# Weight parts written six chunks ahead of an item instead of four (jobs not counted), and the splits of output tiles queued behind the newest parts

## The chip, the cores and the metric

The kernel runs on one core of a Trainium2 chip. The metric is the device time of one execution in microseconds. Three runs of the kernel before gave 2260.38, 2260.41 and 2262.13 us; the median is 2260.41.

The engines are named as in the profile: PE is TensorE (matmuls), with its weight loads shown apart as PEld; DVE is VectorE, ACT is ScalarE, POOL is GpSimd and SP is SyncE, which here only issues DMAs. Each engine works through its own instructions in the order in which they were queued. An instruction that waits holds back all that stands behind it on that engine.

## The reference

Two residual layers on 256 tokens of width 2048, all in float32. The first mixes tokens by neighbourhood attention, the second by a short gated convolution; each is followed by a gated MLP with a convolution of three taps ahead of the gate.

```python
def short_conv_mixer(x, w_in, conv_w, w_out):
    gb, gc, h = jnp.split(x @ w_in, 3, axis=-1)
    return (gb * dwconv_centered(gc * h, conv_w)) @ w_out
...
def conv_glu_ffn(x, w_up, conv_w, conv_b, w_down):
    h = dwconv_centered(x @ w_up, conv_w) + conv_b
    g, u = jnp.split(h, 2, axis=-1)
    return (jax.nn.silu(g) * u) @ w_down
...
    for i in range(DEPTH):
        m, j = i % N_MIXERS, i // N_MIXERS
        a = rms_norm(h, mix_norm[i])
        if m == 0:
            mixed = neighborhood_attention(a, na_w_qkv[j], na_rpb[j], na_w_o[j])
        elif m == 1:
            mixed = short_conv_mixer(a, sc_w_in[j], sc_conv_w[j], sc_w_out[j])
...
        h = h + mixed
        h = h + conv_glu_ffn(rms_norm(h, ffn_norm[i]), ffn_w_up[i], ffn_conv_w[i],
                             ffn_conv_b[i], ffn_w_down[i])
    return rms_norm(h, final_norm)
```

## The kernel before

**Numbers as two parts.** A float32 value goes through PE as the sum of two parts in the type fp32r: `hi` is the value cast down, `lo` is the rest. A weight chunk is 128x1024 numbers (512 KB). It is loaded by SP into a `raw` buffer (line 164), cast on ACT into `hi` (line 185) and subtracted on DVE into `lo` (line 188). There are six buffers each of `raw`, `hi` and `lo`. Each activation tile is split in the same way by `split_into` (ACT cast at line 294, DVE subtraction at line 295).

**Phases.** `Phase` computes products whose output is laid out features by tokens: the q and k columns (`wqk`), the short convolution's inputs (`wsc`), and the MLP's up projections (`wup`), in two halves for each layer. An item is a pair of output tiles, of four chunks in all. PE does 32 matmuls on `hi` (line 262, 512 columns, since both parts of the activation lie side by side) and 32 on `lo` (line 270, 256 columns). When a tile's sum is complete, `evac` takes it out of PSUM: ACT copies half of it (line 315), DVE adds and scales (lines 316 and 321), then come the convolution (ACT line 329, twice DVE line 331), for the first tile of a pair the gate's Silu (ACT line 735), for the second the product (DVE line 738), and the split of the product (lines 294 and 295). `Tokens` computes the products whose output is laid out tokens by features (`wo`, `wscout`, `wdown`), with a scheme of seven products in place of eight for some blocks. That scheme needs sums of activations, which `make_forms` computes on POOL (lines 516 to 519) and splits, and sums of weights.

**Jobs.** The sums of weights are made ahead of time, in the phases before: a job loads three tiles (SP), adds them (DVE, lines 207 to 209) and stores three sums to DRAM (ACT queue, line 214). Jobs stand in the list of chunks between the chunks of the pairs, one behind most pairs of a phase from an early pair on (`hosts`). They count as one chunk each.

**What sets the order.** The main loop goes through the items. `prep_to(n)` writes down load, cast and subtraction of all chunks up to number n. Before an item it is called up to the item's last chunk; after the item, whose `evac` has then been written down, it is called again up to four chunks behind the item's end:

```python
            prep_to(ends[item[0]])
            done = ph.run(ft, c, k0, ka, kb)
...
                prep_to(ends[item[0]] + AHEAD)
```

A scheduler then builds the queue of each engine from this text: an instruction that was written down earlier goes first where several could run by the scheduler's own estimate of time, and later ones go ahead where the earlier ones are not ready by that estimate. `tc.issue_after(x)` adds the one rule that an instruction stands behind `x` on the same engine, without a wait. `load` uses it, so that SP's loads keep the order in which they are written down.

Of the kernel before, what the change touches and what calls it, by code (L numbers as in the profile page):

```python
# [15 lines left out]
F32 = mybir.dt.float32  # L16
# [16 lines left out]
QSCALE = float(128 ** -0.5)  # L33

CH = 8
AHEAD = 4

INTRO = 4
STEP = 4
# [40 lines left out]
def trunk(ctx, tc, xT, par, bias, wqk, wv, wo, wsc, wscout, wup, wdown, out):  # L80
    nc = tc.nc
# [42 lines left out]
    ends = []  # L124
    chunks = []
# [4 lines left out]
    def prep_to(n):  # L130
        while len(prepped) < min(n, len(chunks)):
            src, w, kind = chunks[len(prepped)]
            for due in [x for x in stores if x[0] <= len(prepped)]:
                stores.remove(due)
                due[1]()
            if kind == "make":
                make(*src)
                prepped.append(())
                continue
            raw = wp.tile([P, CH * P], F32, name="raw", tag="raw", bufs=RAWS)  # L140
            if kind == "rows":
                load(raw[:, :w], src)
                prepped.append(parts(raw[:, :w]) + (raw,))
                continue

            if kind == "kept":
                t42, left, sums = prepped[-1][2], prepped[-2][2], src()
                load(t42[:, 4 * P:], sums[:, 8 * P:])
                load(raw, sums[:, :8 * P])
                nc.vector.tensor_add(out=t42[:, :4 * P].rearrange("p (f c) -> p f c", f=4),  # L150
                                     in0=t42[:, 4 * P:].rearrange("p (f c) -> p f c", f=4),
                                     in1=left.rearrange("p (f k c) -> p k f c", f=4, c=P)[:, 1])
                prepped.append((parts(raw), parts(t42)))
                continue

            load(raw[:, :4 * w].rearrange("p (f c) -> p f c", f=4), src.rearrange("f p c -> p f c"))
            prepped.append(parts(raw[:, :4 * w].rearrange("p (f k c) -> p f k c", f=4, c=P)) + (raw,))

    def load(out, in_, strict=True):

        with ExitStack() as order:
            if "SP" in newest:
                order.enter_context(tc.issue_after(newest["SP"].ins))
            last = nc.sync.dma_start(out=out, in_=in_)
        if strict:
            newest["SP"] = last

    def parts(r):

        both, low = high_part(r)  # L170
        low()
        return both
# [15 lines left out]
            newest["DVE"] = nc.vector.tensor_sub(out=lv, in0=r, in1=hv.bitcast(F32))  # L188
        return (hi, lo), low

    kept, newest = {}, {}

    def make(w, g, i, sets, strict):

        kept[id(w), g, i] = dst = dp.tile([P, 3, 4 * P], F32, name=f"kept{len(kept)}")
        if len(sets) < 2:
            sets.append([act_tile().bitcast(F32) for _ in range(3)])
        else:
            sets.reverse()
        for x, f, k in zip(sets[-1], (0, 4, 4), (0, 0, 1)):  # L200
            f, k = 8 * g + f, 2 * i + k
            load(x.rearrange("p (f c) -> p f c", f=4), w[f:f + 4, :, k * P:(k + 1) * P].rearrange("f p c -> p f c"), strict)
        l, r, t = sets[-1]

        def adds():
            with tc.issue_after(newest["DVE"].ins):
                nc.vector.tensor_add(out=l, in0=l, in1=r)
                nc.vector.tensor_add(out=r, in0=t, in1=r)
                nc.vector.tensor_add(out=t, in0=l, in1=t)

        def store():
            for n, x in enumerate((l, r, t)):
                with tc.issue_after(newest["ACT"].ins):
                    nc.scalar.dma_start(out=dst[:, n], in_=x)
        stores.append((len(prepped) + ADDS, adds))
        stores.append((len(prepped) + STORES, store))
# [11 lines left out]
    class Phase:  # L228
# [2 lines left out]

        def __init__(self, w, fts, nk, src, evac, intro=0, step=CH, jobs=(), hosts=(0, 1)):
            self.w, self.nk, self.src, self.evac = w, nk, src, evac
            self.ps = {}
            order = [((ft,), [(k0, k0 + step)]) for k0 in range(0, nk, step) for ft in fts[:intro]]
            rest = fts[intro:]

            odd = len(rest) % 2
            order += [(two, [(k0, k0 + CH) for k0 in range(0, nk, CH)])
                      for two in [rest[:odd]] * odd + [rest[i:i + 2] for i in range(odd, len(rest), 2)]]  # L240
            made, (lo, hi) = 0, hosts
            for n, (two, ks) in enumerate(order):
                items.append((self, two, len(chunks), ks[0][0], ks[0][0], ks[-1][1]))
                for ft in two:
                    for k0, k1 in ks:
                        chunks.append((w[ft, :, k0 * P:k1 * P], (k1 - k0) * P, "rows"))
                ends.append(len(chunks))
                while made < min(len(jobs), max(0, -(-len(jobs) * (n + 1 - lo) // (hi - lo)))):
                    chunks.append((jobs[made], 0, "make"))
                    made += 1  # L250

        def run(self, two, c, k0, ka, kb):
            tiles = [[(k, c + (n * (kb - k0) + k - k0) // CH, (k - k0) % CH * P) for k in range(ka, kb)]
                     for n in range(len(two))]

            for n, ft in enumerate(two):
                if n and waiting:
                    tick()
                if ka == 0:
                    self.ps[ft] = pm.tile([P, 2 * S], F32, name="mm", tag="mm")  # L260
                for k, i, o in tiles[n]:
                    nc.tensor.matmul(self.ps[ft], lhsT=prepped[i][0][:, o:o + P], rhs=self.src[k], start=k == 0,  # L262
                                     stop=False)
            for n, ft in enumerate(two):
                if kb - ka > CH:
                    tick()
                    if n:
                        tick()
                for k, i, o in tiles[n]:
                    nc.tensor.matmul(self.ps[ft][:, S:], lhsT=prepped[i][1][:, o:o + P], rhs=self.src[k][:, :S],  # L270
                                     start=False, stop=k == self.nk - 1)
                if kb == self.nk:
                    self.evac(ft, self.ps.pop(ft))
    held, waiting = [], [True]

    later = []
# [4 lines left out]
    item = [0]  # L281
    at = [0]

    def tick():
        due = [x for x in later if x[0] <= at[0]]
        later[:] = [x for x in later if x[0] > at[0]]
        for _, fn in due:
            fn()
        at[0] += 1


    def split_into(hi, lo, src):

        first = nc.scalar.copy(out=hi, in_=src)  # L294
        nc.vector.tensor_sub(out=lo, in0=src, in1=hi.bitcast(F32))  # L295
        return first

    def split(dst, src):
        return split_into(dst[:, :S], dst[:, S:], src)
# [609 lines left out]
    for item[0], (ph, ft, c, k0, ka, kb) in enumerate(items):  # L909

        with ExitStack() as order:
            for x in factor_at:
                order.enter_context(tc.issue_after(x.ins))
            prep_to(ends[item[0]])
            done = ph.run(ft, c, k0, ka, kb)
            if item[0] != KT // STEP * INTRO:

                if done:
                    order.enter_context(tc.issue_after(done.ins))
                prep_to(ends[item[0]] + AHEAD)  # L920
        if item[0] > KT // STEP * INTRO:
            factor_at.clear()
        tick()
# [70 lines left out]
```

## Time and profile before

| | |
|---|---|
| median of three runs | 2260.41 us |
| the profiled execution: own time / span | 2261.52 / 2259.5 us |
| DVE, busy share of the span | 82% |
| ACT, busy share of the span | 58% |
| POOL, busy share of the span | 5% |
| mean granted PE clock | 0.984 |
| HBM traffic, mean | 245 GB/s |

The order of the work over the span: q, k and v with the attention up to some 320 us, `wo` to some 390 us, the first MLP's halves from there to some 1150 us, each an up phase and a `Tokens` phase; the short convolution to some 1500 us; the second MLP to the end. The share of a busy PE is only half an answer, since a PE that runs at a lower clock is busy too. A view by windows gives the granted clock (PEclk) beside the busy time, and a slower clock is also to be seen in the length of a group of equal matmuls.

### The profile page before, as it was taken

The page shows a single profiled execution, that of the slowest core. Times are in us where ns is not written, and L with a number is a line of the kernel's source. Part 1 is how long each engine was busy: PE and PEld are TensorE (multiplying, and loading weights), DVE is VectorE, ACT ScalarE, POOL GpSimd, SP SyncE. Part 2 cuts the span into 40 slices and gives each one's busy share as a digit, 9 for nine tenths or more (in the row PEclk, how much of TensorE's full clock was granted, in tenths as well). Part 3 has the DMA queues.
Part 4 walks back from the last instruction along what each step waited for, and adds up shares of the span by engine and source line. Part 5 has one row for each costly group of instructions (what it writes and reads, how often), then busy time and mean ns, then how long its engine had stood idle before and what let it go on. Part 6 is the DMA issues. An engine that isn't in the chain of part 4 may idle for free.

```text
span 2259.5 us, 33424 instructions
## 1 busy us (share of the span) xinstructions
PE 2197.4 (97%) x11716; PEld 1902.7 (84%) x11716; DVE 1850.5 (82%) x2842; ACT 1303.6 (58%) x1985; POOL 119.1 (5%) x155
## 2 busy tenths in 40 slices
PE   9999999899999979999999999997999999899998
PEld 8888888778888868888888888886888888788886
DVE  8788668779988868988887877886898887788887
ACT  7555555546666645566655554664666655556565
POOL 1000000002100001210000000000010000000000
PEclk9999999999999989999999999998999999899999
DMA  8678556589768859967778886774986786797685
GB/s 291 222 240 269 182 186 216 170 275 303 258 204 261 268 184 347 315 225 233 255 242 288 300 289 222 233 254 146 315 274 190 247 277 208 255 311 254 196 261 168
DMA packets 362072, 555.34 MB, mean 246 GB/s; under 512 B 21680, under 2 KB 249136, under 8 KB 361904
## 3 DMA queue, kind: packets, MB, share of 16 engines
q1 hardware_dynamic: 332880, 502.23, 68.2%
q10 hardware_dynamic: 29024, 50.98, 5.9%
q8 instruction: 92, 1.51, 0.3%
q14 instruction: 76, 0.62, 0.1%
HBM read 500.70 MB, written 52.43 MB: 245 GB/s over the span
## 4 chain that ended last, share of the span: by engine, by line
PE 94%; DVE 3%; ACT 2%; issue 1%; DMA 0%; POOL 0%; SPq 0%; DVEq 0%; ACTq 0%
PE mm L262 41%; PE mm L270 20%; PE mm L454 6%; PE mm L453 6%; PE mm L455 6%; PE mu L453 3%; PE mu L454 3%; PE mu L455 3%; PE mm L679 1%; PE mm L681 1%; PE mm L680 1%; DVE conv L331 1%; PE tr L361 1%; ACT hi L185 1%; DVE lo L188 1%
## 5 line engine op out<-in xcount | busy, mean ns | idle before, releaser
L185 ACT CAST hi<-raw 128x1024 fp32r<-128x1024 f32 (+1 forms) x920 | 915.0, 1011 | 379.1 <-PE mm L455 127.3
L188 DVE TENSOR_TENSOR lo<-raw,hi 128x1024 fp32r<-128x1024 f32 (+1 forms) x856 | 1015.9, 1212 | 131.8 <-ACT hi L185 61.9
L262 PE MATMUL mm<-a,hi 128*128 128x512 f32 x4096 | 979.8, 396 | 51.4 <-ACT hi L185 50.9
L262 PEld LDWEIGHTS mm<-a,hi 128*128 128x128 f32 x4096 | 772.6, 191 | 210.5 <-ACT hi L185 53.2
L270 PEld LDWEIGHTS mm<-a,lo 128*128 128x128 f32 x4096 | 513.3, 192 | 12.1
L270 PE MATMUL mm<-a,lo 128*128 128x256 f32 x4096 | 518.9, 283 | 0.0
L453 PE MATMUL mm<-hi,act 128*128 128x512 f32 x634 | 247.4, 390 | 0.0
L455 PE MATMUL mm<-hi,act 128*128 128x512 f32 x634 | 246.8, 389 | 0.0
L454 PE MATMUL mm<-lo,act 128*128 128x512 f32 x576 | 224.5, 390 | 0.0
L315 ACT COPY corr<-mm 128x256 f32<-128x256 f32 x256 | 91.1, 370 | 207.4 <-PE mm L270 206.4
L331 DVE SCALAR_TENSOR_TENSOR conv<-pad,pt,conv 128x256 f32<-128x256 f32 x384 | 181.6, 479 | 32.3 <-ACT conv L329 28.0
L329 ACT ACTIVATE conv<-pad,pt 128x256 f32<-128x256 f32 x176 | 105.5, 601 | 163.2 <-DVE pad L321 162.1
L316 DVE TENSOR_TENSOR corr<-mm,corr 128x256 f32<-128x256 f32 x256 | 106.5, 416 | 68.8 <-ACT corr L315 68.1
L455 PEld LDWEIGHTS mm<-hi,act 128*128 128x128 f32 x634 | 119.1, 188 | 24.6
L453 PEld LDWEIGHTS mm<-hi,act 128*128 128x128 f32 x634 | 119.1, 188 | 24.4
L454 PEld LDWEIGHTS mm<-lo,act 128*128 128x128 f32 x576 | 108.2, 188 | 21.8
L519 POOL TENSOR_TENSOR s<-conv 128x128 f32<-128x128 f32 x27 | 39.6, 1468 | 1079.2 <-DVE conv L738 1079.2
L295 DVE TENSOR_TENSOR act<-conv,act 128x256 fp32r<-128x256 f32 x88 | 37.2, 423 | 54.5 <-ACT act L294 54.3
L321 DVE TENSOR_TENSOR pad<-corr,rstd 128x256 f32<-128x256 f32 x176 | 73.7, 419 | 0.8
L454 PE MATMUL mu<-lo,sf 128*128 128x512 f32 x180 | 70.1, 389 | 0.0
L455 PE MATMUL mu<-hi,sf 128*128 128x512 f32 x180 | 70.1, 389 | 0.0
L453 PE MATMUL mu<-hi,sf 128*128 128x512 f32 x180 | 70.1, 389 | 0.0
(160 smaller groups left out, 1573.0 us busy)
## 6 DMA issues: line engine op xcount, KB each, us to landing
raw<-in_wup SPq DMA_DIRECT2D x352, 512.0 KB, 5.5
raw<-in_wdown SPq DMA_DIRECT2D x124, 512.0 KB, 4.8
kept<-act ACTq DMA_DIRECT2D x192, 256.0 KB, 4.9
raw<-in_wsc SPq DMA_DIRECT2D x96, 512.0 KB, 5.5
act<-in_wdown SPq DMA_DIRECT2D x156, 256.0 KB, 6.0
raw<-kept SPq DMA_DIRECT2D x64, 512.0 KB, 5.0
raw<-in_wqk SPq DMA_DIRECT2D x56, 512.0 KB, 4.9
raw<-in_wv SPq DMA_DIRECT2D x32, 512.0 KB, 4.4
```

What stands on the lines that cost most here:

```text
L185: newest["ACT"] = nc.scalar.copy(out=hv, in_=r)
L188: newest["DVE"] = nc.vector.tensor_sub(out=lv, in0=r, in1=hv.bitcast(F32))
L262: nc.tensor.matmul(self.ps[ft], lhsT=prepped[i][0][:, o:o + P], rhs=self.src[k], start=k == 0, stop=False)
L270: nc.tensor.matmul(self.ps[ft][:, S:], lhsT=prepped[i][1][:, o:o + P], rhs=self.src[k][:, :S], start=False, stop=k == self.nk - 1)
L315: nc.scalar.copy(out=corr, in_=ps[:, S:])
L316: nc.vector.tensor_add(out=corr, in0=ps[:, :S], in1=corr)
L321: nc.vector.tensor_mul(out=dst, in0=both(ps), in1=rstd)
L329: nc.scalar.activation(c, x[:, 1:S + 1], AF.Identity, scale=w[1], bias=b)
L331: nc.vector.scalar_tensor_tensor(out=c, in0=x[:, tap:tap + S], scalar=w[tap], in1=c, op0=ALU.mult, op1=ALU.add)
L453: nc.tensor.matmul(ps, lhsT=xh, rhs=wh, start=start, stop=False)
L454: nc.tensor.matmul(ps, lhsT=xh, rhs=wl, start=False, stop=False)
L455: nc.tensor.matmul(ps, lhsT=xl, rhs=wh, start=False, stop=stop)
```

## The change

`AHEAD` becomes 6, and it now counts chunks of weights alone: jobs in between are written down too, but don't use up the count. Besides, the splits that an `evac` of a `Phase` writes down for its finished output tile (all phases but `wqk`), those of `make_forms` among them, are queued behind the newest `hi` cast on ACT and the newest `lo` subtraction on DVE that were written down before them.

```diff
-AHEAD = 4
+AHEAD = 6
...
-    kept, newest = {}, {}
+    kept, newest, fenced = {}, {}, []
...
-            self.ps = {}
+            self.ps, self.fence = {}, w is not wqk
...
                 if kb == self.nk:
+                    if self.fence:
+                        fenced.append(True)
                     self.evac(ft, self.ps.pop(ft))
+                    fenced.clear()
...
     def split_into(hi, lo, src):
 
-        first = nc.scalar.copy(out=hi, in_=src)
-        nc.vector.tensor_sub(out=lo, in0=src, in1=hi.bitcast(F32))
+        with ExitStack() as order:
+            if fenced:
+                for x in ("ACT", "DVE"):
+                    order.enter_context(tc.issue_after(newest[x].ins))
+            first = nc.scalar.copy(out=hi, in_=src)
+            nc.vector.tensor_sub(out=lo, in0=src, in1=hi.bitcast(F32))
         return first
...
-                prep_to(ends[item[0]] + AHEAD)
+                end, n = ends[item[0]], AHEAD
+                while n and end < len(chunks):
+                    n -= chunks[end][2] != "make"
+                    end += 1
+                prep_to(end)
```

The lines of the changed kernel are shifted: 301, 302, 322, 323, 328, 336, 742 and 745 are the lines 294, 295, 315, 316, 321, 329, 735 and 738 of before.

Three places show what moves.

**First place: ACT, the first pair with a job in the first up phase.** In these rows `mm` is the PSUM tile of an output tile, `corr` its copy, `kept7` the first job's sums. Before, `mm_4542` is the second tile of the pair that PE finishes here, and `hi_4635` and `hi_4641` are the first two chunks of the next pair.

```order
L315 COPY corr_4601<-mm_4542 128x256
L735 ACTIVATE g_4583<-conv_4579 128x256
L329 ACTIVATE conv_4605<-pad2_85,pt_79 128x256
L294 CAST act_4610<-conv_4605 128x256
L294 CAST sf_4618<-s_4613 128x3x128
L294 CAST act_4498<-s_4613 128x128
L185 CAST hi_4635<-raw_4633 128x1024
L185 CAST hi_4641<-raw_4639 128x1024
```

In the changed kernel the same pair is `mm_4547` and `mm_4564`, and the next pair's chunks are `hi_4537`, `hi_4543`, `hi_4650` and `hi_4656`.

```order
L322 COPY corr_4597<-mm_4547 128x256
L185 CAST hi_4537<-raw_4535 128x1024
L336 ACTIVATE conv_4601<-pad1_84,pt_79 128x256
L185 CAST hi_4543<-raw_4541 128x1024
L322 COPY corr_4623<-mm_4564 128x256
L214 DMA kept7_4525<-act_4526 128x512
L214 DMA kept7_4525<-act_4527 128x512
L742 ACTIVATE g_4605<-conv_4601 128x256
L214 DMA kept7_4525<-act_4528 128x512
L336 ACTIVATE conv_4627<-pad2_85,pt_79 128x256
L185 CAST hi_4650<-raw_4648 128x1024
L185 CAST hi_4656<-raw_4654 128x1024
```

The next pair's first two casts have moved from behind the splits of the finished pair to behind the copy of its first tile; its last two stand ahead of those splits as well.

**Second place: ACT, one pair later.** Before, `mm_4677` is the second tile of the pair that PE finishes, and `hi_4760` the first chunk of the next one.

```order
L315 COPY corr_4736<-mm_4677 128x256
L735 ACTIVATE g_4718<-conv_4714 128x256
L329 ACTIVATE conv_4740<-pad1_84,pt_79 128x256
L294 CAST act_4745<-conv_4740 128x256
L185 CAST hi_4760<-raw_4758 128x1024
L185 CAST hi_4766<-raw_4764 128x1024
```

In the changed kernel this pair is `mm_4682` and `mm_4699`, the next pair's first chunks are `hi_4672` and `hi_4678`, and the fenced splits of the pair before (`act_4632`, `sf_4640`, `act_4510`) stand here.

```order
L322 COPY corr_4732<-mm_4682 128x256
L301 CAST act_4632<-conv_4627 128x256
L301 CAST sf_4640<-s_4635 128x3x128
L301 CAST act_4510<-s_4635 128x128
L336 ACTIVATE conv_4736<-pad0_83,pt_79 128x256
L322 COPY corr_4758<-mm_4699 128x256
L742 ACTIVATE g_4740<-conv_4736 128x256
L185 CAST hi_4672<-raw_4670 128x1024
```

`hi_4672` now stands behind the copy of the second tile and the first tile's Silu, no longer behind the second tile's convolution and split. What the Silu waits for is seen on DVE of the changed kernel, where `conv_4627` is the product of the pair before, `lo_4657` the last chunk of the current one, and `act_4661` to `act_4663` the second job's tiles.

```order
L745 TENSOR_TENSOR conv_4627<-conv_4627,g_4605 128x256
L188 TENSOR_TENSOR lo_4657<-raw_4654,hi_4656 128x1024
L302 TENSOR_TENSOR act_4632<-conv_4627,act_4632 128x256
L302 TENSOR_TENSOR sf_4640<-s_4635,sf_4640 128x3x128
L302 TENSOR_TENSOR act_4510<-s_4635,act_4510 128x128
L323 TENSOR_TENSOR corr_4732<-mm_4682,corr_4732 128x256
L328 TENSOR_TENSOR pad0_83<-corr_4732,rstd_82 128x256
L207 TENSOR_TENSOR act_4661<-act_4661,act_4662 128x512
L338 SCALAR_TENSOR_TENSOR conv_4736<-pad0_83,pt_79,conv_4736 128x256
L208 TENSOR_TENSOR act_4662<-act_4663,act_4662 128x512
L338 SCALAR_TENSOR_TENSOR conv_4736<-pad0_83,pt_79,conv_4736 128x256
```

The first tile's convolution (`conv_4736`) stands behind the splits of the pair before and between two of the job's additions.

**Third place: SP at the start**, from its third load on (`in_xT` is the input, two tiles of 128 features a load; a count stands behind equal rows). Before:

```order
L868 DMA act<-in_xT 128x512
L164 DMA raw<-in_wqk 128x512 x4
L868 DMA act<-in_xT 128x512
L164 DMA raw<-in_wqk 128x512
L868 DMA act<-in_xT 128x512
```

In the changed kernel:

```order
L875 DMA act<-in_xT 128x512
L164 DMA raw<-in_wqk 128x512 x6
L875 DMA act<-in_xT 128x512
L164 DMA raw<-in_wqk 128x512
L875 DMA act<-in_xT 128x512
```

Two more weight loads, the sixth and the seventh, stand ahead of the third and fourth loads of the input. From the first up phase on SP's queue holds the same loads in the same order as before.

## The prediction

> **What bounds the kernel now.** I read the page's busy times first, then the waits of PE, then PE's windows and its timeline.
>
> ```profile
> PE 2197.4 (97%) x11716; PEld 1902.7 (84%) x11716; DVE 1850.5 (82%) x2842; ACT 1303.6 (58%) x1985; POOL 119.1 (5%) x155
> ...
> PE mm L262 <- ACT hi L185: 50.9, 11, 7.0
> ...
> 800.00:850.00 50.00, 37.79 (x188) 32.28 (x187) 32.34 (x53) 18.69 (x30) 1.97 (x4) 0.83 0.47 155
> ```
>
> PE is the bound: it idles 62 us of 2259.5. Of these, 50.9 are waits for the cast of a weight chunk (line 185), in eleven pieces. They come in clusters, and in such a window the granted clock falls too (0.83, the last but two of the columns). The timeline shows the pieces of one cluster, and the only single one:
>
> ```profile
> 820.30 10.46 PE L262 MATMUL mm<-a,hi 128*128 128x512 f32 x32 [6.95 <-ACT hi L185]
> ...
> 839.85 9.29 PE L262 MATMUL mm<-a,hi 128*128 128x512 f32 x32 [5.26 <-ACT hi L185]
> ...
> 1202.81 7.57 PE L262 MATMUL mm<-a,hi 128*128 128x512 f32 x32 [1.57 <-ACT hi L185]
> ```
>
> The same two-stall cluster stands at 448, 820, 1551 and 1923 us: the start of each of the four up phases, at its first two pairs with a job. Together: 4 x 12.2 + 1.6 = 50.4 us; the other two pieces are the kernel's first matmuls. The chain of work shows what a stall costs on top, in the length of 32 equal matmuls (the first row is undisturbed; then the first and the last cluster):
>
> ```profile
> 419.19 7.28 PE mm L262 x32
> ...
> 448.36 10.39 PE mm L262 x32
> 467.83 9.26 PE mm L262 x32
> ...
> 1923.00 10.37 PE mm L262 x32
> 1942.46 9.25 PE mm L262 x32
> ```
>
> After the long stall 3.1 us more than 7.28, after the second 2.0, after the single one of 1.57 us 0.3. With the two clusters between (5.2 and 4.7) that makes 20.4 us. Stalls and slow matmuls: **70.8 us** that are not PE's own work.
>
> Why does PE wait? The chain from the end of a pair to the next one (start, length):
>
> ```profile
> 809.52 1.93 PE mm L270 x16
> ...
> 811.47 0.38 ACT corr L315
> ...
> 811.88 0.44 DVE corr L316
> ...
> 812.34 0.44 DVE pad L321
> ...
> 812.86 0.61 ACT conv L329
> ...
> 813.49 0.48 DVE conv L331
> ...
> 814.74 0.35 ACT g L735
> ...
> 816.81 0.43 DVE conv L738
> ...
> 817.31 0.46 POOL s L516
> ...
> 818.47 0.52 ACT sf L294
> ...
> 819.21 1.05 ACT hi L185
> ```
>
> The next pair's first cast comes behind the whole evacuation of the pair before, down to POOL's sums and their split. The data was not what was late:
>
> ```profile
> 790.05 4.26 SPq L164 DMA_DIRECT2D raw<-in_wup  x4
> ...
> DMA to landing us min/median/max: 3.6/5.9/8.1
> ...
> 811.47 0.37 ACT L315 COPY corr<-mm 128x256 f32<-128x256 f32 x1 [5.10 <-PE mm L270]
> ```
>
> These four loads are the pair's chunks: issued by 794.3, landed by some 802 at the latest, cast from 819.21 on. ACT sat idle 5.1 us meanwhile, waiting for the copy at the head of its queue. It is the place in ACT's queue that costs, and the queue of before (first and second place of the change) shows just that place at all nine stalls.
>
> **The change part by part.**
>
> *First stall of a cluster.* The next pair's first cast now stands behind the copy of the finished pair's first tile. What that chain costs can be read at the single stall, which has copy and cast alone ahead of PE:
>
> ```profile
> 1201.45 0.36 ACT corr L315
> 1201.81 0.95 ACT hi L185
> ```
>
> From the end of PE's sum to its next matmul that was the 1.57 us above. But the first tile is complete 1.92 us (16 matmuls of line 270, half of 3.83) before PE wants the cast. 1.57 < 1.92: no stall. I take 0; bounds 0 and 0.5. The pair's other casts: I set t = 0 at the first tile's end, so that the next pair starts at 1.92. ACT does copy, cast, convolution, cast until 3.1; DVE does copy's sum, scaling, two subtractions of 1.22 and two steps of the convolution until 4.8, then sum and scaling of the second tile until 5.6; ACT's convolution follows until 6.3, then the casts of chunks three and four, done at 7.25 and 8.2. The scheduler now has PE finish the first tile before it starts the second (16 matmuls of 0.23, 16 of 0.12), which wants chunk three at 1.92 + 3.64 + 1.92 = 7.48. Just in time.
>
> *Second stall.* Here something remains. DVE reaches the product (line 738, now 745) at 8.4. What follows it was seen once in the same arrangement, with the subtraction of a chunk right behind the product:
>
> ```profile
> 882.44 0.42 DVE L738 TENSOR_TENSOR conv<-conv,g 128x256 f32<-128x256 f32 x1
> 882.78 1.22 DVE L188 TENSOR_TENSOR lo<-raw,hi 128x1024 fp32r<-128x1024 f32 x1
> ...
> 882.94 1.71 POOL L516 TENSOR_TENSOR s<-conv 128x128 f32<-128x128 f32 x1 [8.73 <-DVE conv L738]
> ...
> 885.22 0.51 ACT L294 CAST sf<-s 128x384 fp32r<-128x384 f32 x1 [1.91 <-POOL s L517]
> ...
> 886.44 1.22 DVE L188 TENSOR_TENSOR lo<-raw,hi 128x1024 fp32r<-128x1024 f32 x1
> ...
> 819.70 0.68 DVE L207 TENSOR_TENSOR act<-act 128x512 f32<-128x512 f32 x1
> ```
>
> POOL's first sum took 1.71 us beside that subtraction, against 0.46 in the stall. DVE was free of the splits 4.0 us after the product's start: at 12.4. Then come sum and scaling of the first tile (scaling from 12.9; ACT's convolution 0.5 later, at 13.4), a step of the convolution (0.6 after ACT's, at 14.0, with the job's first addition in the gap), the second addition, the second step (at 15.0). Silu starts 0.5 later, the cast of the next pair's first chunk at 15.8, PE 1.09 after that (819.21 to 820.30): 16.9. PE had ended the pair at 1.92 + 7.28 + 3.83 = 13.0. **Stall: 3.9 us.** Lower bound: the Silu is ready early, and the cast waits for copy and Silu only: 1.57 + 0.4 = 2.0. Upper bound: the second stall as it was, 5.26.
>
> Slow matmuls after it: between 0.3 (1.57 us) and 2.0 (5.26 us); on the line between them, 0.3 + 2.3 x 0.46 = 1.4, which I take. [...]
>
> Per cluster 3.9 + 1.4 = 5.3 remain, **21.2 us** in four. All four clusters have the same rows in ACT's new queue. The single stall goes: its cast stands ahead of the second tile's copy now.
>
> *The fence* adds no instruction and no wait. It puts the splits behind casts that can wait for a buffer of an earlier chunk. Their outputs are read only by the Tokens phase, after the rest of the up phase, so this cover is long; if it were gone, the price is the cast's wait, under 2 us a pair. Two chunks more ahead cost no work either: the counts of casts, subtractions and loads are the same. In the q, k and v phases jobs and bias loads change places with weight loads on SP; PE is busy 50.00 of 50 us in each window from 100 to 400 (one row for all six), and I take 0, with 2 us as upper bound.
>
> ```profile
> 150.00:200.00 50.00, 50.00 (x288) 44.11 (x287) 37.14 (x60) 28.28 (x49) 2.73 (x2) 1.00 0.69 223
> ```
>
> At the starts of three phases the activations have a few matmuls less of cover: 0, upper bound 1.5 in all.
>
> *Start.* The third and fourth loads of the input stand behind two more weight loads, and weight loads from the seventh on wait for a buffer.
>
> ```profile
> 5.54 0.70 SPq L868 DMA_DIRECT2D act<-in_xT  x1
> ...
> 9.29 0.99 SPq L164 DMA_DIRECT2D raw<-in_wqk  x2
> ...
> act<-in_xT SPq DMA_DIRECT2D x8, 256.0 KB, 5.1
> ...
> 13.49 0.89 ACT L302 ACTIVATE a<-act,pt 128x256 fp32r<-128x256 f32 x2
> ...
> 14.56 0.50 PE L262 MATMUL mm<-a,hi 128*128 128x512 f32 x1 [0.27 <-DVE a L303]
> ```
>
> The fourth input load was issued at 5.54. Now the eighth weight load, which was issued at 9.29, goes ahead of it: issue at 9.7, landing 5.1 later at 14.8 in place of ACT's start at 13.49. PE used it at 14.56, already waiting a little; it comes 1.4 later, and some 0.4 of that is covered by matmuls on the third load that now stand ahead. I take **1.0 us**; bounds 0 and 2.5.
>
> *Sum.* 70.8 - 21.2 - 1.0 = 48.6 us. The profiled execution took 2261.5 (span 2259.5): 2212.9. The median of the runs is 1.1 lower: **2212**.
>
> **The rivals.**
>
> *The clock stays up after the short stall*, as it nearly did after the one of 1.57 us: 0.3 in place of 1.4 in each cluster, 4 x 4.2 = 16.8 remain, 2207. For it: 3.9 is not far above 1.57; against it: the 2.0 after a stall of 5.26. [...]
>
> *The short chain*: POOL and DVE are quicker than I laid them end to end, the stall is 2.0 with 0.3 behind it: 4 x 2.3 = 9.2 remain, 2200. For it: the order forces no more than that. Against: 1.71 for POOL's sum in just this arrangement.
>
> *The long chain*: the second stall stays as it was (5.26 + 2.0) and chunk three comes a microsecond late: 4 x 8.3 = 33 remain, 2224; with the start at 2.5, 2225. For it: my chain leaves 0.2 us of room at chunk three.
>
> *Slower*: DVE becomes the bound where jobs run, since its queue now has chunk subtractions, splits and additions waiting for one another in a fixed order.
>
> ```profile
> 550.00:600.00 50.00, 50.00 (x285) 44.11 (x284) 45.39 (x80) 29.90 (x50) 7.64 (x9) 1.00 0.90 293
> ```
>
> DVE is busy 45.39 of 50 there, 10.1 of a pair's 11.1 us, so that 1.0 us of its idling a pair is free. Jobs stand in 44 pairs of up phases and 13 of the short convolution. From 1.0 + 48.6/57 = 1.9 us of idling a pair the gain is gone; at 2.2 it is 57 x 1.2 = 68 us, 2280. Against: POOL and ACT are far from busy, and the same kinds of waits stood in the queue before.
>
> *It doesn't act*: the stalls stay, 2260. The queue's rows speak against it.
>
> **How the numbers follow.** Forecast 0.46, clock up 0.15, short chain 0.13, long chain 0.20, slower 0.04, no effect 0.02. The range reaches from the short chain less 3 us (for a start that costs nothing and for rounding) to the long one with the starts' and the q, k and v phases' upper bounds: 2197 to 2228; it leaves out the last two cases and the tails. A measurement can tell 0.2%, some 4.5 us, from no change: faster 0.94, same 0.02, slower 0.04.
>
> **What would show it.** In the profile of the changed kernel: no stall of PE over 0.5 us at the first pair with a job of each up phase; one of 2 to 5 us, on line 185, a pair later, with Silu (line 742) just ahead of that cast; none near 1200; PE's waits for casts near 16 us in place of 50.9; a microsecond lost before 20 us; POOL's sum over a microsecond in that pair. It is wrong if PE waits at other places, or if two stalls a cluster remain.

## The result, and the profile after

| | before | changed |
|---|---|---|
| median | 2260.82 us (4 runs, 2260.38 to 2262.13) | 2221.63 us (4 runs, 2219.21 to 2222.3) |
| ratio, 95% interval | | 0.9824 (0.9807 to 0.9841) |
| profiled execution, own time / span | 2261.52 / 2259.5 us | 2221.64 / 2219.5 us |
| mean granted PE clock | 0.984 | 0.996 |

The kernel became 39 us faster; 2212 was forecast, with 2197 to 2228 as its range. The kind is right and the size is 9.6 us off. Where these 9.6 us went is the subject of what follows.

The page's busy times and then the waits of PE in the changed kernel (who waits for whom: us in all, times, longest):

```profile
PE 2186.1 (98%) x11716; PEld 1891.2 (85%) x11716; DVE 1852.2 (83%) x2842; ACT 1306.1 (59%) x1985; POOL 128.6 (6%) x155
```

```profile
PE mm L262 <- ACT hi L185: 14.4, 6, 3.4
PE mm L262 <- DVE h L357: 2.4, 2, 1.6
PE tr L639 <- DVE act L302: 1.8, 1, 1.8
PE bc L803 <- DVE conv L801: 1.6, 1, 1.6
PE o L651 <- DVE act L302: 1.2, 2, 1.1
PE mm L460 <- ACT hi L185: 1.2, 1, 1.2
PE mm L270 <- DVE lo L188: 1.1, 1, 1.1
```

The waits for casts fell from 50.9 to 14.4 us. Below them stand small waits that the profile of before did not have, or had shorter: for residual additions (`h`, line 357), for splits in the attention (`act`, line 302; the one of 1.8 was 0.7 before), for a cast in a token phase, for the subtraction of a chunk. The wait of 1.6 at line 803 was there before, equally long. The idle time of PE is 33.4 us in place of 62.1.

The stalls that are left are four, and they are equal (timeline of PE, idle time and releaser in brackets):

```profile
458.53 5.44 PE L262 MATMUL mm<-a,hi 128*128 128x512 f32 x16 [3.39 <-ACT hi L185]
...
818.42 3.94 PE L262 MATMUL mm<-a,hi 128*128 128x512 f32 x16 [3.39 <-ACT hi L185]
...
1542.61 5.53 PE L262 MATMUL mm<-a,hi 128*128 128x512 f32 x16 [3.39 <-ACT hi L185]
...
1902.57 5.34 PE L262 MATMUL mm<-a,hi 128*128 128x512 f32 x16 [3.38 <-ACT hi L185]
```

The four stalls are equal, but what follows them is not: the same 16 matmuls take 3.94 us behind the second and 5.34 to 5.53 behind the others. In the 11.1 us from each stall's end on the granted clock was 0.85, 1.00, 0.85 and 0.86. Each is at the second pair with a job of an up phase. At the first such pair there is none, and none in the short convolution. What stands ahead of the late cast shows ACT's timeline at the third of them, where PE ended the pair at 1539.2:

```profile
1539.06 0.60 ACT L336 ACTIVATE conv<-pad,pt 128x256 f32<-128x256 f32 x1 [1.30 <-DVE pad L328]
1539.57 0.35 ACT L322 COPY corr<-mm 128x256 f32<-128x256 f32 x1
1541.21 0.42 ACT L742 ACTIVATE g<-conv 128x256 f32<-128x256 f32 x1 [1.29 <-DVE conv L338]
1541.53 1.03 ACT L185 CAST hi<-raw 128x1024 fp32r<-128x1024 f32 x1
```

The copy of the second tile, then the Silu, which waits 1.29 us for DVE's convolution, then the cast: the place and the chain that the prediction had named.

**Where the 40 us came from** can be read without any model of PE, by the times at which the same matmul begins in both traces: the first ones of the token phases of the MLPs and of the short convolution, and the last ones of three token phases (before, then changed; 393.99, 1143.03 and 1497.46 are last ones).

```profile
393.99 0.39 PE L455 MATMUL mm<-hi,act 128*128 128x512 f32 x1
658.58 0.40 PE L453 MATMUL mm<-hi,act 128*128 128x512 f32 x1
1030.62 0.40 PE L453 MATMUL mm<-hi,act 128*128 128x512 f32 x1
1143.03 0.39 PE L455 MATMUL mm<-hi,act 128*128 128x512 f32 x1
1414.09 0.40 PE L453 MATMUL mm<-hi,act 128*128 128x512 f32 x1
1497.46 0.39 PE L455 MATMUL mm<-hi,act 128*128 128x512 f32 x1
1761.28 0.40 PE L453 MATMUL mm<-hi,act 128*128 128x512 f32 x1
2133.20 0.40 PE L453 MATMUL mm<-hi,act 128*128 128x512 f32 x1
```

```profile
396.93 0.39 PE L462 MATMUL mm<-hi,act 128*128 128x512 f32 x1
649.13 0.40 PE L460 MATMUL mm<-hi,act 128*128 128x512 f32 x1
1009.51 0.40 PE L460 MATMUL mm<-hi,act 128*128 128x512 f32 x1
1124.82 0.39 PE L462 MATMUL mm<-hi,act 128*128 128x512 f32 x1
1395.35 0.40 PE L460 MATMUL mm<-hi,act 128*128 128x512 f32 x1
1478.98 0.39 PE L462 MATMUL mm<-hi,act 128*128 128x512 f32 x1
1733.28 0.40 PE L460 MATMUL mm<-hi,act 128*128 128x512 f32 x1
2093.06 0.40 PE L460 MATMUL mm<-hi,act 128*128 128x512 f32 x1
```

Subtract line by line, and then each difference from the next one:

| stretch | changed less before, at its end | in the stretch |
|---|---|---|
| start, q, k, v, attention, `wo` | +2.94 | **+2.94** |
| first up phase | -9.45 | -12.39 |
| second up phase (the token phase ahead of it: 0) | -21.11 | -11.66 |
| its token phase | -18.21 | **+2.90** |
| short convolution | -18.74 | -0.53 |
| its token phase | -18.48 | +0.26 |
| third up phase | -28.00 | -9.52 |
| fourth up phase (the token phase ahead of it: 0) | -40.14 | -12.14 |
| last token phase | -39.97 | +0.17 |

Two of the gains contain a loss at the start of their phase: the short convolution had lost 1.32 us (a group of 32 matmuls behind its start begins at 1167.72 before and at 1150.83 now) before it gained 1.85 at the place of its single stall, and the third up phase lost 1.79 (its first matmul begins at 1497.68 and 1480.99). So the stretches with before's nine stalls gained 12.39 + 11.66 + 11.31 + 12.14 + 1.85 = **49.35 us**, where 49.6 was forecast (70.8 - 21.2). Everything else lost 2.94 + 2.90 + 1.32 + 0.26 + 1.79 + 0.17 = **9.4 us**, where 1.0 was forecast. In these two traces that is the miss: 8.4 + 0.25 of the 8.7 us between 48.6 and 39.9 (the profiled executions, 2261.52 and 2221.64). The rest of the 9.6 is the 1.1 us by which the forecast put the median under the profiled execution; the changed kernel's median is its profiled time.

The agreement of 49.35 with 49.6 is closer than it should be. The second up phase's 11.66 is what is left after two new waits of PE far from its cluster, of 0.29 us at 868.97 and this one:

```profile
919.55 1.21 PE L270 MATMUL mm<-a,lo 128*128 128x256 f32 x8 [1.15 <-DVE lo L188]
```

Without these two the nine places gained some 50.8 us, and all that is lost elsewhere comes to 10.8.

### The profile page after: what moved, and what is told of

The parts are those of the page before. It is cut to its first block, busy times and chain, and to the rows that moved or that the text cites. A ratio compares the mean times of both kernels' runs of the same rounds, so it can differ in the third digit from the quotient of the medians.

```text
span 2219.5 us, 33399 instructions
## 1 busy us (share of the span) xinstructions
PE 2186.1 (98%) x11716; PEld 1891.2 (85%) x11716; DVE 1852.2 (83%) x2842; ACT 1306.1 (59%) x1985; POOL 128.6 (6%) x155
## 4 chain that ended last, share of the span: by engine, by line
PE 84%; DVE 6%; DMA 3%; ACT 3%; issue 2%; POOL 1%; SPq 0%; ACTq 0%; DVEq 0%
PE mm L262 35%; PE mm L270 18%; PE mm L460 6%; PE mm L461 6%; PE mm L462 6%; PE mu L460 3%; DVE lo L188 3%; PE mu L461 3%; PE mu L462 3%; DMA raw<-in_wup 2%; ACT hi L185 2%; PE mm L688 1%; PE mm L686 1%; PE mm L687 1%; DVE conv L338 1%
## 5 line engine op out<-in xcount | busy, mean ns | idle before, releaser
L262 PE MATMUL mm<-a,hi 128*128 128x512 f32 x4096 | 970.9, 392 | 17.3 <-ACT hi L185 14.4
L262 PEld LDWEIGHTS mm<-a,hi 128*128 128x128 f32 x4096 | 761.3, 189 | 172.6 <-ACT hi L185 18.1
L338 DVE SCALAR_TENSOR_TENSOR conv<-pad,pt,conv 128x256 f32<-128x256 f32 x384 | 182.1, 479 | 26.4 <-ACT conv L336 21.2
```

Of the source, the lines that this page charges most:

```text
L338: nc.vector.scalar_tensor_tensor(out=c, in0=x[:, tap:tap + S], scalar=w[tap], in1=c, op0=ALU.mult, op1=ALU.add)
```

## The experiments

Each ran beside the kernel before on the same chip; the medians of that kernel lay between 2260.36 and 2260.57 us. Each figure is a median of four runs.

**e1: the second part of the change taken away.**

```diff
-            self.ps, self.fence = {}, w is not wqk
+            self.ps, self.fence = {}, False
```

> The changed kernel without its second part: the splits of output tiles are not queued behind the newest casts and subtractions; six chunks ahead, jobs not counted, stays. Theory (all of the effect is the two chunks ahead; the casts stand where they stand because they are written down earlier): the time stays, 2221.6 us within 2, with the same four stalls of 3.39 us at the second pair with a job and PE idle 33 us. Rival (the second part is what frees the casts from the splits): the splits go back ahead of the casts, stalls at the first pair with a job come back, 4 x (7.0 + 3.1) = 40 us, towards 2260.

Measured: 2221.22 us, ratio 0.9825 (0.981 to 0.984). The theory holds, and more strictly than it was put: without the rule the instructions of all five engines stand in the very same order as with it. The rule that a split stands behind the newest casts is kept anyway. The change is its two more chunks and nothing else.

So e1 is also the changed order executed once more, and its trace, laid beside the one of before in the same way, shows which of the losses come back. Up to the end of `wo` it lost 3.94 us (2.94 in the first trace), at the two phase starts 1.60 and 1.43 (1.32 and 1.79). But the token phase of the first MLP's second half lost 0.55 in place of 2.90, and the two waits in the second up phase are not there. Outside the nine places it lost 8.2 us in all. The losses in the attention and at the phase starts belong to the order; the 2.90 and the two waits come in one execution of it and not in the other.

**e2: six ahead only after pairs**, so that the stretches that lost go back to four.

```diff
-                end, n = ends[item[0]], AHEAD
-                while n and end < len(chunks):
-                    n -= chunks[end][2] != "make"
-                    end += 1
-                prep_to(end)
+                if getattr(ph, "fence", False) and len(ft) == 2:
+                    end, n = ends[item[0]], AHEAD
+                    while n and end < len(chunks):
+                        n -= chunks[end][2] != "make"
+                        end += 1
+                    prep_to(end)
+                else:
+                    prep_to(ends[item[0]] + 4)
```

> Six chunks ahead (jobs not counted) only after items that are pairs of the short convolution and of the up phases; after all other items (q, k, v, the token phases, and the single tiles with which a phase begins) four, jobs counted, as before. Theory (what is missing from the forecast is lost outside the clusters, where the two more chunks ahead put weight casts and subtractions in front of work that PE waits for: 2.9 us up to the end of q, k and v, 2.9 in the token phase of the first MLP's second half, 3.1 at the two phase starts behind it and 0.4 elsewhere, 9.3 in all): these go and the four stalls stay, 2221.6 - 9.3 = 2212.3. Rival (these waits come from what the removed stalls let run earlier, loads and jobs, whatever is written ahead in those phases): 2221.6 less the 2.9 of q, k and v, which lie ahead of the first stall: 2218.7.

Measured: 2213.41 us, ratio 0.9795 (0.9778 to 0.9811), 8.2 below the changed kernel. The theory said 9.3 below, the rival 2.9. The four stalls are still there (3.31 to 3.39), and the small waits are gone: against before, the first up phase begins 0.36 us earlier in place of 2.94 later, and at the two phase starts nothing is lost. The token phase of the second half loses 0.44 in place of 2.90, which tells little beside the 0.55 of e1. Between the two profiled runs the difference is 11.5 us in place of 8.2: the one of e2 was the fastest of its four.

What the two chunks do there shows best at the end of the short convolution's token phase. In the changed kernel PE waited 1.62 us for a residual addition (1480.99 in the timeline of PE). The timelines of ACT and of DVE ahead of that:

```profile
1473.92 1.05 ACT L185 CAST hi<-raw 128x1024 fp32r<-128x1024 f32 x1 [1.23 <-DMA raw<-in_wup]
1476.14 1.05 ACT L185 CAST hi<-raw 128x1024 fp32r<-128x1024 f32 x1 [1.17 <-DMA raw<-in_wup]
```

```profile
1475.01 1.23 DVE L188 TENSOR_TENSOR lo<-raw,hi 128x1024 fp32r<-128x1024 f32 x1 [0.56 <-ACT hi L185]
1477.22 1.23 DVE L188 TENSOR_TENSOR lo<-raw,hi 128x1024 fp32r<-128x1024 f32 x1 [0.99 <-ACT hi L185]
...
1480.16 0.68 DVE L357 TENSOR_TENSOR h<-mm,h 128x512 f32<-128x512 f32 x1
```

Two casts of the next phase's chunks wait for their loads; two subtractions wait for those casts; the residual additions, whose sums PE had long finished, stand behind them on DVE. The same place in e2, on DVE and then on PE (the phase's last matmul and the next phase's first ones):

```profile
1461.57 2.35 DVE L188 TENSOR_TENSOR lo<-raw,hi 128x1024 fp32r<-128x1024 f32 x2
...
1465.64 0.68 DVE L357 TENSOR_TENSOR h<-mm,h 128x512 f32<-128x512 f32 x1
```

```profile
1468.47 0.39 PE L462 MATMUL mm<-hi,act 128*128 128x512 f32 x1
1468.69 1.52 PE L262 MATMUL mm<-a,hi 128*128 128x512 f32 x6
```

Here the same addition ends at 1466.3, 2.4 us before PE begins the next phase, and PE doesn't wait. In the attention the casts wait for PE in place of a load (that it is PE's release of a buffer is likely, but the trace doesn't say so). ACT in the changed kernel, ahead of PE's wait of 1.05 us at 171.75:

```profile
167.50 2.00 ACT L185 CAST hi<-raw 128x1024 fp32r<-128x1024 f32 x2 [1.38 <-PE o L653]
169.41 0.36 ACT L301 CAST act<-o 128x256 fp32r<-128x256 f32 x1
```

The attention's split stands behind two casts. Before, the same split waited 0.34 us for PE's own result (at 166.23 us) and for nothing else, and PE didn't wait there.

**e3: six ahead also after the single tiles at a phase's start.** The condition of e2 without its second half.

```diff
-                if getattr(ph, "fence", False) and len(ft) == 2:
+                if getattr(ph, "fence", False):
```

> Six chunks ahead (jobs not counted) after all items of the short convolution and of the up phases, the single tiles at a phase's start among them; four, jobs counted, after items of q, k, v and of the token phases. Theory (each loss sits where its own chunks are written ahead): the 2.9 us of q, k and v and the 2.9 of the token phase go, the 3.1 at the phase starts stay, since they come from the chunks written behind the single tiles there: 2215.6 to 2216. Rival (the phase starts lose by the last items of the token phase ahead of them, which now write four again): they go too, 2212.3. Rival from below (nothing but q, k and v is bound to its own chunks): 2218.7.

Measured: 2215.1 us, ratio 0.9799 (0.9785 to 0.9814). By its time this is the theory; by its trace it is the rival, and the trace decides. PE has no wait for a residual addition at either phase start, and from the end of the token phase to the end of the short convolution 1.71 us are gained, the 1.85 of the single stall less 0.14. The two medians differ by 1.7 us, and the runs overlap (2212.49 to 2217.74 against 2210.09 to 2215.24). The two profiled runs differ by 3.9, and there the difference lies in PE's clock behind the first two stalls, which were equally long in both (windows of 11.1 us from the first two stalls' ends on: length, PE's busy time, granted clock, DMA share, GB/s). e3, then e2:

```profile
455.48:466.58 11.10, 11.10 (x44) 0.74 0.89 297
816.51:827.61 11.10, 11.10 (x51) 0.86 0.85 293
```

```profile
455.57:466.67 11.10, 11.10 (x63) 1.00 0.92 308
813.97:825.07 11.10, 11.10 (x63) 1.00 0.88 292
```

So the losses at the phase starts came from the chunks written behind the last items of the token phase, as in the rows of e2, not by those behind the single tiles; as to the medians it is likely, not shown, that the clock makes up their difference too.

**e4: the Silu behind the newest cast.**

```diff
-                nc.scalar.activation(g, c, AF.Silu)
+                with tc.issue_after(newest["ACT"].ins):
+                    nc.scalar.activation(g, c, AF.Silu)
```

> The changed kernel with one edit: the Silu of a pair's first tile stands behind the newest cast of a chunk on ACT. At the second pair with a job the next pair's first cast then has the copy of the second tile ahead of it, and no longer the Silu with the DVE chain that it waits for. Theory A (the place in ACT's queue is what lasts, with the load of the chunk close behind it as the next limit: in the profile of the changed kernel the load was issued 5.8 us ahead of PE's restart in the first cluster, 7.1 in the second, over 9 in the third and 6.7 in the fourth; with the 4.9 from issue to landing and 1.05 from the cast's start to PE that leaves stalls of 3.4, 2.3, 1.6 and 2.6): 9.9 us of stalls in place of 13.6, and the slow matmuls behind them down by 1 to 3 us: 2215 to 2217. Theory B (the data is late and the Silu only happens to end then): 3.4 in all four, 2221.6. Theory C (the queue alone): 1.6 to 2.0 in all four and hardly a slow matmul, 2209 to 2211.

Measured: 2212.59 us, ratio 0.979 (0.9776 to 0.9805), 9.0 below the changed kernel. Theory A had read the wrong loads. Counted from the start of the run, the cast that PE waits for in the first cluster belongs to the first load of this group of the changed kernel (SP's timeline):

```profile
431.35 15.72 SPq L164 DMA_DIRECT2D raw<-in_wup  x4
```

It was issued 27 us ahead of PE's restart; the loads named in the expectation belong to later chunks. The stalls are equal in all four clusters, 1.67 to 1.69 us, so the queue alone is the limit (theory C). Of its price one part was missing: the second cast of the pair now stands behind a convolution that waits for DVE, and a second stall of 1.23 to 1.24 follows. Together that is 2.9 in place of 3.39 a cluster, 1.9 us in four. Some 4.9 us more are the clock of the profiled runs, which fell behind three of the changed kernel's four stalls (to 0.85, 0.85 and 0.86) and behind none of these shorter ones (first cluster, 1.00):

```profile
456.49:467.59 11.10, 9.87 (x51) 1.00 0.90 296
```

What remains of the 10.1 us between the two spans, some 3 us, lies outside the clusters, in small waits that were shorter in this execution, as in e1's.

**e5: e2 with the tiles' copies behind the newest cast.**

```diff
-        nc.scalar.copy(out=corr, in_=ps[:, S:])
+        with ExitStack() as order:
+            if fenced:
+                order.enter_context(tc.issue_after(newest["ACT"].ins))
+            nc.scalar.copy(out=corr, in_=ps[:, S:])
```

> The kernel of e2 (six ahead only after pairs) with one edit: in the short convolution and the up phases, the copy of a finished tile stands on ACT behind the newest cast of a chunk that is written down. The first two casts of the next pair then stand ahead of both copies of the pair that PE is finishing, so that no cast in ACT's queue waits for PE to end the pair ahead of it. Theory (what is left of the clusters is the place behind the second tile's copy and the Silu; the chunk itself has long landed, as e4's equal stalls in all four clusters say): the four stalls of 3.4 us and the slow matmuls behind them (none to 2.9 us each in e2) go: 2213.4 - 13.5 - 4 to 6 = 2194 to 2196. Rival 1 (the data): if a load was the next limit behind the queue, stalls of some 1 to 3 us stay in clusters where jobs' loads stand ahead: 2197 to 2206. Rival 2 (the evacuation becomes late: the copies wait for two casts of 1.05, DVE's sums, splits and additions come 2 us later in every pair, and PE waits for subtractions): 0.3 us in 57 pairs is 17 us, 2211 or more.

Measured: 2199.19 us, ratio 0.9727 (0.971 to 0.9743). All four stalls are gone and PE has no wait for a cast of line 185 left. But the gain falls short of the forecast by some 4 us. In the profiled run, which at 2203.24 us was the slowest of the four, PE now waits for subtractions, and these waits are all in the second half of the first MLP, where a job stands behind each of 13 pairs in a row. The waits of PE, the chain of work ahead of one of these waits (start, length), and the busy time of DVE around it by windows of 20 us (length, busy, granted clock, DMA share, GB/s):

```profile
PE mm L270 <- DVE lo L188: 8.1, 4, 3.8
```

```profile
843.98 8.93 DMA kept<-act
...
853.97 6.78 DMA raw<-in_wup
860.75 0.27 DVE act L302
861.01 2.27 DVE lo L188 x2
...
864.62 1.14 DVE lo L188
```

```profile
840.00:860.00 20.00, 13.10 (x22) 1.00 0.93 297
860.00:880.00 20.00, 17.67 (x31) 1.00 0.93 308
```

A job's store takes 8.9 us from issue to landing, SP's next load waits for that, and a chunk's load behind it takes 6.8 more; the DMA engines are busy 0.93 of the time. DVE idles in 6.9 of the first 20 us. So it is neither the data of the stalled casts (rival 1) nor a late evacuation in every pair (rival 2), but the transfers of the densest stretch of jobs. The changed kernel lost 1.4 us in the same stretch (0.29 and 1.15), the kernel before nothing.

**e6: five chunks ahead; e7: six with jobs counted.** Both from the changed kernel.

```diff
-AHEAD = 6
+AHEAD = 5
```

```diff
-                end, n = ends[item[0]], AHEAD
...
-                prep_to(end)
+                prep_to(ends[item[0]] + AHEAD)
```

> The changed kernel with five chunks ahead in place of six (jobs not counted), in all phases. Theory (the clusters turn on one chunk: with the next pair's first cast written down ahead of the evacuation it stands where it stands with six; the losses outside grow with what is written ahead): the first stalls and the single one go as with six, four stalls of 3.39 stay, and of the 9.3 us lost outside the clusters about half is lost: 2215 to 2218. Rival 1 (both chunks are needed: the second cast still stands behind the evacuation): stalls of 3 to 5 us come back at the second chunk, 2235 or more. Rival 2 (the losses outside come with the first chunk ahead, or not from the number at all): 2221.6.

> The changed kernel with jobs counted again: six entries of the list ahead, of which a job is one. Theory (behind a pair with a job that still leaves five chunks, so the first cast of the next pair stands where it stands now; behind all others nothing changes): the time stays, 2221.6 within 2, four stalls of 3.39. Rival (not counting the jobs is what frees the casts in the stretches with jobs): the clusters come back in part, 2235 or more.

Measured: e6 2217.22 us, ratio 0.9805 (0.9791 to 0.982); e7 2221.09 us, ratio 0.9826 (0.9812 to 0.9841). Both times are the theories': four stalls of 3.37 to 3.42 in each, and none at the first pairs. One chunk beyond four does all that the change does for the stalls; not counting the jobs does nothing that can be measured. With five, the waits at the phase starts are gone, but nothing is saved in the attention: its waits reach 2.54, and e6 is 4.0 us late at the end of `wo`. Some of the token phase's remain. That the losses grow with what is written ahead is thus not shown.

**e8: e5 with the jobs of the MLPs' second halves spread over more pairs.**

```diff
-                  jobs=take(UP_JOBS[2 * layer + half]), hosts=(3, 16) if half else (8, 22))
+                  jobs=take(UP_JOBS[2 * layer + half]), hosts=(3, 20) if half else (8, 22))
```

> The kernel of e5 with the jobs of the second up phase of each MLP spread over the pairs 3 to 20 in place of 3 to 16. Theory (what e5 still waits for, 8.1 us of subtractions of chunks between 850 and 940 us, comes from transfers: there a job stands behind every pair, the DMA engines are busy 0.93 to 1.05 of the time, and the chain leads from a job's stores over the loads behind them to the subtraction): with fewer jobs to a pair these waits go or fall under 2 us: 2199.2 - 6 to 8 = 2191 to 2193. Rival 1 (DVE itself is the bound there, by the fixed order of its queue and not by transfers): the work of a job is the same wherever it stands, and the waits stay as many: 2199. Rival 2 (the last jobs come too late: the sums that they store are read at the start of the token phase): new waits at the token phases, 2202 or more.

Measured: 2190.72 us, ratio 0.9692 (0.9676 to 0.9708), runs from 2190.28 to 2191.1: the fastest of all, 30.9 us below the changed kernel. No wait for a subtraction is left, nor a new one in a token phase. Spreading also thins DVE's work per pair, so that e8 by itself doesn't tell DVE from the transfers; DVE's idle time in e5 does.

## Why the prediction was right, and where its size failed

- **The bound and the cause** (the place of the casts in ACT's queue, not the data) hold. e4 and e5 move only places in that queue, and the stalls follow, down to none.
- **First stall of a cluster: 0.** So in all four. The single stall went as well: 1.85 us gained, 1.57 + 0.3 forecast.
- **Second stall: 3.9 + 1.4.** The step is right, its size a little too long. It is 3.39, and behind it the clock cost 0 to 1.7 us (windows at 0.85, 1.00, 0.85 and 0.86 of the clock). The chain was laid in the right order and half a microsecond too long: the Silu came 15.0 us after the first tile's end, not 15.5. Part of that was POOL's first sum:

```profile
450.83 1.37 POOL L523 TENSOR_TENSOR s<-conv 128x128 f32<-128x128 f32 x1 [13.63 <-DVE conv L745]
```

  It took 1.37 us beside a subtraction of a chunk, where 1.71 was taken over from before. The clock's price was no straight line here: the 0.3 us that the forecast took for slow matmuls behind the single stall were not the clock, which was 1.00 in the 11.1 us behind it. That the line's 1.4 lies near the four measured losses (4.9 us, 1.2 each) is luck. For all nine places together 49.6 us was forecast, and some 50.8 came.
- **The fence: "adds no instruction and no wait."** True, but the sentence behind it, that it puts the splits behind the casts, is wrong: e1 shows that it places nothing.
- **"Two chunks more ahead cost no work either"** is the step that failed. The work is indeed the same, but two more chunks' casts and subtractions stand in front of what PE needs next. In the q, k and v phases 0 was taken (bound 2), and 2.7 was lost, at three places in the attention: 1.14 at the split of 69.61, 0.32 by 98 and 1.20 at the split of 171.75. At the phase starts 0 was taken (bound 1.5 in all), and 1.32 + 1.79 was lost. Both bounds were too low. The token phases were not looked at, and cost 2.90 + 0.26 + 0.17 in this execution, though far less in e1's. e2 takes the cause away: in its trace all this together comes to nothing, and its median is 8.2 us lower. The evidence used was the wrong kind: a PE that is busy 50.00 of 50 us shows that nothing was late, not by how little. At the place of the 1.62 us wait the margin of the four-ahead order was 2.4 us (e2's rows), the price of two chunk subtractions. What stays open is why the attention lost only 0.8 us in e7 (from 0.46 early at 64 to 0.34 late at the end of `wo`), with six entries ahead.
- **The start: 1.0.** It cost nothing that can be measured. Ahead of the first wait in the attention, the matmul that began at 64.15 before begins at 64.43. At that place the five kernels with the new order of loads (the changed one, e1, e4, e6, e7) are between 0.46 us early and 0.28 late, the four that start like before (e2, e3, e5, e8) 0.1 to 0.3 early.
- **The range and the signs.** That the range held is in part luck: its upper end came from the long chain, which didn't happen, and not from the losses that did. Of the signs named, all but one came: there is no microsecond lost before 20 us. And PE does wait at other places, which the prediction had named as a sign of being wrong: its account of the clusters stands, its account of the rest doesn't.
- **The rivals.** The short chain (2200), the long one (2224), the slower case and "no effect" were not what happened; the time fell between the forecast and the long chain, by another mechanism than either. The rival in which the clock stays up came true in one cluster of four (granted clock 1.00 behind the second stall). DVE as the bound, the slower case, is not seen even in e5: there DVE idles 6.9 of 20 us while it waits for transfers of 8.9 and 6.8 us.

## What to carry to other kernels

A queue position has two sides: writing work down earlier frees it from what stood ahead (here PE's waits for casts fell from 50.9 to 14.4 us), and puts it ahead of something else (here PE then waited 1.62 us for a residual addition), so each phase has to be asked what now stands behind it, even where the profile shows no wait. Where an engine's cover is to be trusted, read its margin (when the needed result ended against when it was wanted), not the busy share. And confine such a change to the stretch whose stall it cures: here pairs alone gave 8 us more, and the copies behind the casts with the jobs spread another 23.

## What the runs showed of the hardware

In these profiles the clock that PE lost behind a stall fell into three groups, and stalls of one length fell into all three. The same stall of 3.31 to 3.42 us was seen 24 times in six kernels (the changed one, e1, e2, e3, e6, e7). In the 11.1 us behind it the granted clock was 1.00 seven times, 0.85 to 0.87 twelve times, and 0.73 to 0.75 five times: that is 0, about 1.6 (11.1 x 0.14) and about 2.9 us (11.1 x 0.26) lost. The mean of these is 1.4, the prediction's value, which came from a straight line: luck. All of e4's eight stalls between 1.2 and 1.7 us left the clock at 1.00; all four of 5.26 in the kernel before brought 0.83 to 0.85, and all four of 6.9 brought 0.72 to 0.75. The profiled runs of e2 and e3 differ by little else: 2210.09 against 2214.02 us. Whether this difference also makes the spread between the runs of one kernel is not shown: e8, without a stall of PE over 2 us, spreads over 0.8 us in four runs, and e7 and e6, with four of 3.4 each, over 2.1 and 6.8; but e4, whose stalls left the clock at 1.00 in its profiled run, spreads over 4.2.
